# Two decoder blocks in split float32r on one core: pools divided so that matmul operands start at multiples of 128 bytes

## The chip, the cores and the metric

The kernel runs on one NeuronCore of a Trainium2 chip. The metric is the device time of one execution in microseconds (us), as the median of the runs of a kernel. TensorE (PE), VectorE (DVE), ScalarE (ACT) and GpSimd (POOL) compute; SyncE (SP) issues the DMAs.

## The reference

Two transformer blocks follow each other over 256 tokens of width 1024. The first has two layers (a low-rank attention beside a dilated attention, then a block attention), each with a feed-forward part of width 4096 and a gated projection. The second has two layers over the 256 tokens and, in its first layer, 256 context tokens: a gated convolution, an attention and a gated linear attention side by side, three branch projections and an output projection. All of it is float32, and nearly all of the arithmetic is products of a 256-row activation with weight matrices:

```python
h = x
for i in range(DEPTH):
    hn = rms_norm(h, mix_norm[i])
    mix = even_mixer(hn, ...) if i % 2 == 0 else odd_mixer(hn, ...)
...
def odd_mixer(hn, w_in, qn, kn, w_out):
    z = (hn @ w_in).reshape(B, S, 3, MOBA_HEADS, HEAD_DIM)
...
    return o.reshape(B, S, ODD_MIX) @ w_out
```

## The kernel before

**A product in three passes.** Every float32 operand of a large product is held as a pair of float32r tiles, a rounded part `hi` and the remainder `lo`. `mm3` (lines 295 to 299) multiplies a pair by a pair with three matmuls into one PSUM bank, on lines 297, 298 and 299:

```python
        mm(ps, sl, mh, start=first, stop=False)
        mm(ps, sh, ml, start=False, stop=False)
        mm(ps, sh, mh, start=False, stop=last)
```

The second argument of `mm` is the stationary operand (loaded into the array, 128 columns), the third the moving one (streamed through it). The profile names the moving operand first: `mm<-xh,wlo` streams `xh` past the loaded `wlo`.

**Weights.** `unit` (L263) loads up to 1 MB of a weight matrix into a `raw` tile; ACT rounds it into `whi` (L280) and DVE subtracts to get `wlo` (L281), 1024 columns at a time. There are three `raw` buffers and four each of `whi` and `wlo`. PE multiplies one unit while the next ones are loaded and split.

**Two shapes.** `gemm_nat` (L301) keeps a 128x128 piece of the activation stationary and streams 512 (or 384, 288) weight columns; its operands appear as `mm<-whi,xl` and `mm<-wlo,xh`. `gemm_tr` (L326) and `tr_mm` (L286) keep a 128x128 piece of the weight stationary and stream 256 activation columns, `mm<-xh,wlo`. In the second block some weights multiply both token groups at once, with 512 moving activation columns. `branches2` (L1641) is the end of a layer of the second block: it streams `ph` and `pl` (256 columns) past the branch weights, and holds `sh` and `sl` stationary against `w_out_2`.

**Order.** The order of the work is written out by generators: `run` (L1742) interleaves steps of the first block with filler steps of the second by declared costs, and `block2` (L1713) runs the second block's layers. SP issues the weight loads in the order in which PE will use them. This order is fixed when the program is built and does not depend on where a tile lies.

**Where tiles lie.** Every tile comes from a pool, and pools lie one behind another in each partition's memory. Within a pool the tiles lie one behind another, each rounded up to a multiple of 32 bytes. The weight pool `w` comes first and starts at a multiple of 128; each of its tiles is 8192 or 4096 bytes. Next is `const`, which begins with `cols`, 193 floats or 772 bytes, taking 800; everything behind it is shifted by 32 bytes, and further small tiles shift it again. The first block's tiles come from `b1` (and `fill`), the second block's from `d0`, `d1` (`dense2`) and `b0`, `b1` (`branches2`). The start of a tile past a multiple of 128 bytes, in the kernel before:

| tiles | pool | bytes past a multiple of 128 |
|---|---|---|
| `raw`, `whi`, `wlo` | `w` | 0 |
| `ident` | `const` | 32 |
| `xh`, `xl` | `xq` | 64 |
| `E0`, `E1` (in rows: `E`) | first block | 64 |
| `E2`, `E3` (in rows: `E`) | first block | 0 |
| `ph`, `pl`, `sh`, `sl` | `branches2` | 96 |
| `T` tiles, `vvh`, `vvl`, `kTh`, `kTl` | `dense2` | 0, 32, 64 or 96 |

A slice that a matmul reads starts a multiple of 512 bytes inside its tile, so it has the same offset as the tile. Of the large products, `E2` with `E3` against weights has both operands at 0; no product with 256 moving columns has.

Of the kernel before, what the change touches and what calls it, by code (L numbers as in the profile page):

```python
# [10 lines left out]
F32 = mybir.dt.float32  # L11
# [9 lines left out]
P = 128  # L21
# [113 lines left out]
for _n, _k in COLS:  # L135
    COFF[_n] = _o
    _o += _k
NCOL = _o

ROWS = [("e_qn_nope", 64), ("e_qn_rope", 32), ("e_kn_nope", 64), ("e_kn_rope", 32),  # L140
        ("q_norm_g_2", 256), ("k_norm_g_2", 256)]
# [55 lines left out]
        self.hi, self.lo = hi, lo  # L197


class Kern:  # L200
    def __init__(self, tc, ins, out, ctx, dbg=None):
        self.tc, self.nc, self.i, self.out, self.dbg = tc, tc.nc, ins, out, dbg or {}
        pool = lambda n, b, **k: ctx.enter_context(tc.tile_pool(name=n, bufs=b, **k))
        self.wp = pool("w", 3)
        self.cp = pool("const", 1)
        xq = pool("xq", 1)
        self.xs = [xq.tile([P, 2, 8, 256], F32R, name=f"x{n}") for n in "hl"]
        self.zp = pool("zp", 1)
        self.ps = pool("ps", 1, space=PSUM)
        self.nuid = 0  # L210
        self.pre = PRE
# [933 lines left out]
    def evacs(self, l, s, T):  # L1145

        nc, V, A = self.nc, self.nc.vector, self.nc.scalar

        def conv(c):
            st = {}  # L1150

            def e_c(ps):
                st["v"] = T("cv", [P, 2, 256])
                A.copy(st["v"], ps)

            def e_x(ps):
                v = st["v"]
                u = T("cu", [P, 2, 258])
                nc.gpsimd.memset(u[:, :, 0:1], 0.0)
                nc.gpsimd.memset(u[:, :, 257:258], 0.0)  # L1160
                V.tensor_tensor(u[:, :, 1:257], ps, v, op=OP.mult)
                for j in range(2):
                    w = [self.col("conv_w_2", (l * 3 + k) * 8 + c * 2 + j) for k in range(3)]
                    A.mul(v[:, j], u[:, j, 0:256], w[0])
                    V.scalar_tensor_tensor(v[:, j], u[:, j, 1:257], w[1], v[:, j], op0=OP.mult, op1=OP.add)
                    V.scalar_tensor_tensor(v[:, j], u[:, j, 2:258], w[2], v[:, j], op0=OP.mult, op1=OP.add)

            def e_b(ps):
                V.tensor_tensor(st["v"], ps, st["v"], op=OP.mult)

            def e_z(ps):
                z = T("zt", [P, 2, 256])
                A.activation(z, ps, AF.Tanh, scale=0.5)
                V.scalar_tensor_tensor(z, z, 1.0, ps, op0=OP.add, op1=OP.mult)
                V.scalar_tensor_tensor(z, z, 0.5, st["v"], op0=OP.mult, op1=OP.mult)
                self.spill(l, s, "conv", c * 2, z)
            return [(c0 + c * 256, e) for c0, e in ((1024, e_c), (2048, e_x), (0, e_b), (3072, e_z))]

        def silu(name, c):

            def e(ps):
                z = T("zt", [P, 2, 256])
                for o, q in zip([z[:, a] for a in range(2)], ps) if isinstance(ps, list) else [(z, ps)]:
                    A.activation(o, q, AF.Tanh, scale=0.5)
                    V.scalar_tensor_tensor(o, o, 1.0, q, op0=OP.add, op1=OP.mult)
                self.spill(l, s, name, c * 2, z)
            return e

        def gate(j, c):

            def e(ps):
                z = T("zt", [P, 2, 256])
                for a in range(2):
                    A.activation(z[:, a], ps[a] if isinstance(ps, list) else ps[:, a], AF.Tanh, scale=0.5,
                                 bias=self.col("b_gate_2", l * 24 + j * 8 + c * 2 + a))
                self.spill(l, s, f"g{j}", c * 2, z)
            return e
        return {"conv": conv, "silu": silu, "gate": gate}
# [514 lines left out]
    def block2(self, dram, xs_dram):  # L1713
        nc, i = self.nc, self.i
        tc = self.tc
        self.bg, self.credit = [], 0.0
        xp = {0: self.xp0, 1: self.xp1}
        for l in range(2):
            def T(tag, shape, bufs=1, dt=F32):
                self.nuid += 1  # L1720
                return self.dp.tile(shape, dt, name=f"{tag}_{l}_{self.nuid}", tag=tag, bufs=bufs)
            self.rate = RATE[l]
            with tc.tile_pool(name=f"d{l}", bufs=1) as self.dp:
                self.lmask = T("lmask", [P, MASKS, P], dt=I32)
                self.rope2 = T("T9", [P, 2, 2, P])
                nc.sync.dma_start(self.rope2, i["c_rope2"].rearrange("p (c t d) -> p c t d", c=2, t=2))
                nc.sync.dma_start(self.lmask, i["c_lmask"].rearrange("p (a b) -> p a b", a=MASKS))
                mats = self.load(T("T8", [P, 4, P]), i["c_mats"].rearrange("p (a b) -> p a b", a=4))
                self.matsr = T("matsr", [P, 4, P], dt=F32R)
                nc.vector.tensor_copy(self.matsr, mats)  # L1730
                self.dense2(l, xp[0], xp[1])
            with tc.tile_pool(name=f"b{l}", bufs=1) as self.dp:
                ctx_in = self.branch_input(0, 1, 0, T) if l == 0 else None
                x = self.post2(l, 0, *self.branches2(l, 0, T, after=ctx_in), xs_dram[0][l], T, xs_dram[0][l + 1])
                self.dump(f"x{l}", x)
                if l == 0:
                    xp[0] = self.norm2(1, 0, x, T)
                    x = self.post2(0, 1, *self.branches2(0, 1, T, ready=ctx_in), xs_dram[1][0], T)
                    xp[1] = self.norm2(1, 1, x, T)
                    self.conv_units(1, [(0, xp[0])])  # L1740

    def run(self):  # L1742
        nc, i, tc = self.nc, self.i, self.tc
        with tc.tile_pool(name="dram", bufs=1, space=bass.MemoryType.DRAM) as dram:
            tok = lambda a: a.rearrange("(t p) d -> p t d", p=P)
            dt = lambda n: dram.tile([P, 2, D], F32, name=n)
            xs_dram = {0: {0: dt("xl0"), 1: dt("xl1"), 2: tok(self.out)}, 1: {0: tok(i["ctx_2"])}}
            with tc.tile_pool(name="b1", bufs=1) as big, tc.tile_pool(name="fill", bufs=1) as fp:
                self.big, self.fp = big, fp
                self.scr = {(l, s, n): dram.tile([P, 8, 256], F32, name=f"scr{l}{s}{n}")  # L1750
                            for l in range(2) for s in range(2 - l) for n in ("conv", "att", "gla", "za", "zg", "g0", "g1", "g2")}
                self.cz = {n: dram.tile(sh, F32, name=f"cz_{n}") for n, sh in
                           (("k", [P, 2, 512]), ("q", [P, 2, D]), ("gk", [P, 2, 512]), ("gv", [P, 2, D]), ("gq", [P, D]), ("r", [32, 256]))}
                h = self.sb("h", [P, 2, D])
                self.load_consts()
                for b in range(2):
                    for t in range(2):
                        nc.sync.dma_start(h[:, t, b * 512:(b + 1) * 512], tok(i["x"])[:, t, b * 512:(b + 1) * 512])
                    if b == 0:
                        nc.sync.dma_start(self.cols, i["cols"])  # L1760
                        self.first = self.unit(i["e_w_in"], 0, 2, 0, 384)
                self.gdram = [dram.tile([2, D], F32, name=f"gdram{l}") for l in range(2)]

                rest = chain(self.ada(0), self.ada(1))

                def filler():
                    for _ in range(9):
                        yield next(rest)
                    yield from self.ctx_proj(xs_dram[1][0])
                    yield from rest  # L1770
                f = filler()
                turn = 0
                debt = 0.0
                for pe, lat in self.block1(h):
                    if self.ph == "ff0":
                        turn += 1
                        if turn % AT == 0:
                            next(rest, None)
                    debt += lat * LATF
                    while debt > 0:  # L1780
                        d = next(f, None)
                        if d is None:
                            debt = -1e9
                        else:
                            debt -= d
                for _ in f:
                    pass
                nc.sync.dma_start(xs_dram[0][0], h)
            self.block2(dram, xs_dram)
# [21 lines left out]
```

## Time and profile before

| | |
|---|---|
| median of 3 runs | 2135.53 us (2134.28 to 2136.55) |
| the profiled execution | 2133.83 us, of which the span is 2132.1 us |
| PE, matmuls | busy 98% of the span |
| DVE, ACT, POOL | busy 71%, 53%, 0% |
| DMA | 55.4% of 16 engines' time, 186 GB/s in the mean |
| TensorE's granted clock | 0.996 |

The span runs from the first to the last instruction. "Busy" for PE counts a matmul from its start to its modelled end, and matmuls overlap: one of 256 columns lasts some 0.28 us in the profile while the next starts 0.11 us after it. So the busy share says little of how fast PE runs. What counts is the distance from one start to the next, which the timeline shows: the difference between the starts of the first and the last matmul of an unbroken stretch, divided by their number less one. The chain of work that ended last tells which engine's time sets the end.

### The profile page before, as it was taken

Reading aid. Unit: us, or ns where it says so; the run is one execution under the profiler, and the core shown is the slowest. Engines: PE = TensorE matmul, PEld = TensorE weight load, DVE = VectorE, ACT = ScalarE, POOL = GpSimd, SP = SyncE. Lnnn points to the kernel's source line nnn. Section 1 sums busy time; section 2 is a strip of 40 time slices with the busy share of each in tenths; the row PEclk is TensorE's granted clock in tenths of the full one; section 3 lists DMA queues with packets and bytes.
Section 4 is the critical chain, followed back from the end, with each engine's and each line's share of the span. In section 5 each row is a group of like instructions: output and inputs, shape, how many; then the busy total and the mean of one; then the engine's idle time right before and its main releaser. Section 6 shows DMA issues by size and latency. Waiting matters only on the chain.

```text
span 2132.1 us, 34406 instructions
## 1 busy us (share of the span) xinstructions
PE 2092.7 (98%) x13618; PEld 1863.3 (87%) x13618; DVE 1516.2 (71%) x2837; ACT 1120.5 (53%) x1790; POOL 8.4 (0%) x42
## 2 busy tenths in 40 slices
PE   7999999999999999999999999999999999999998
PEld 5788878888999888989998888889899988989997
DVE  6875556677767657998898567347878677668676
ACT  4654434465555445666565545434546445747543
POOL 0000000000000000000000000000000000000000
PEclk9999999999999999999999999999999999999999
DMA  7744687555435555744633343568865631425695
GB/s 265 249 152 166 229 279 275 188 182 189 140 127 178 196 183 193 258 161 139 205 119 118 107 139 113 201 234 276 277 227 192 217 126 65 137 92 159 210 314 178
DMA packets 282154, 397.48 MB, mean 186 GB/s; under 512 B 12676, under 2 KB 189156, under 8 KB 279560
## 3 DMA queue, kind: packets, MB, share of 16 engines
q1 hardware_dynamic: 281992, 395.28, 55.4%
q8 instruction: 107, 1.75, 0.3%
q14 instruction: 55, 0.45, 0.1%
HBM read 363.21 MB, written 32.03 MB: 185 GB/s over the span
## 4 chain that ended last, share of the span: by engine, by line
PE 85%; DVE 6%; DMA 4%; ACT 4%; issue 1%; SPq 0%; DVEq 0%; ACTq 0%
PE mm L298 24%; PE mm L299 24%; PE mm L297 24%; DVE wlo L281 2%; PE tp L1590 2%; DMA raw<-in_w_ff 1%; PE at L1608 1%; PE at L1425 1%; ACT whi L280 1%; PE at L1539 1%; PE at L582 1%; DMA lp<-scr01za 1%; PE tp L1442 1%; PE mm L949 1%; PE at L297 1%
## 5 line engine op out<-in xcount | busy, mean ns | idle before, releaser
L281 DVE TENSOR_TENSOR wlo<-raw,whi 128x1024 fp32r<-128x1024 f32 (+1 forms) x572 | 690.5, 1211 | 321.8 <-ACT whi L280 319.6
L280 ACT CAST whi<-raw 128x1024 fp32r<-128x1024 f32 (+1 forms) x572 | 592.0, 1041 | 487.1 <-PE mm L299 338.2
L297 PE MATMUL mm<-xh,wlo 128*128 128x256 f32 (+2 forms) x2048 | 619.0, 302 | 4.6 <-DVE wlo L281 4.3
L298 PE MATMUL mm<-xl,whi 128*128 128x256 f32 (+2 forms) x2048 | 616.3, 301 | 0.9 <-DVE xl L406 0.9
L299 PE MATMUL mm<-xh,whi 128*128 128x256 f32 (+2 forms) x2048 | 614.7, 300 | 0.0
L297 PEld LDWEIGHTS mm<-xh,wlo 128*128 128x128 f32 (+1 forms) x2048 | 382.6, 187 | 29.1 <-DVE wlo L281 8.3
L299 PEld LDWEIGHTS mm<-xh,whi 128*128 128x128 f32 (+1 forms) x2048 | 383.6, 187 | 14.2
L298 PEld LDWEIGHTS mm<-xl,whi 128*128 128x128 f32 (+1 forms) x2048 | 382.7, 187 | 15.0 <-DVE xl L406 1.1
L298 PE MATMUL mm<-wlo,xh 128*128 128x512 f32 (+3 forms) x704 | 268.7, 382 | 4.4 <-DVE wlo L281 4.4
L297 PE MATMUL mm<-whi,xl 128*128 128x512 f32 (+3 forms) x704 | 267.1, 381 | 4.9 <-ACT whi L280 4.8
L299 PE MATMUL mm<-whi,xh 128*128 128x512 f32 (+3 forms) x704 | 265.9, 378 | 0.0
L297 PE MATMUL mm<-ph,wlo 128*128 128x256 f32 x576 | 162.7, 282 | 0.0
L298 PE MATMUL mm<-pl,whi 128*128 128x256 f32 x576 | 162.6, 282 | 0.0
L299 PE MATMUL mm<-ph,whi 128*128 128x256 f32 x576 | 162.6, 282 | 0.0
L297 PEld LDWEIGHTS mm<-whi,xl 128*128 128x128 f32 x704 | 133.5, 190 | 31.8 <-ACT whi L280 8.0
L298 PEld LDWEIGHTS mm<-wlo,xh 128*128 128x128 f32 x704 | 134.4, 191 | 28.0 <-DVE wlo L281 6.3
L299 PEld LDWEIGHTS mm<-whi,xh 128*128 128x128 f32 x704 | 134.2, 191 | 23.1
L298 PE MATMUL mm<-wlo,E 128*128 128x512 f32 (+1 forms) x292 | 113.7, 389 | 0.6 <-DVE wlo L281 0.6
L297 PE MATMUL mm<-whi,E 128*128 128x512 f32 (+1 forms) x292 | 113.5, 391 | 0.0
L299 PE MATMUL mm<-whi,E 128*128 128x512 f32 (+1 forms) x292 | 113.4, 388 | 0.0
L297 PEld LDWEIGHTS mm<-ph,wlo 128*128 128x128 f32 x576 | 109.2, 190 | 0.2 <-DVE wlo L281 0.2
L298 PEld LDWEIGHTS mm<-pl,whi 128*128 128x128 f32 x576 | 109.3, 190 | 0.1
(449 smaller groups left out, 2827.9 us busy)
## 6 DMA issues: line engine op xcount, KB each, us to landing
raw<-in_w_in SPq DMA_DIRECT2D x130, 1024.0 KB, 5.2
raw<-in_w_ff SPq DMA_DIRECT2D x64, 1024.0 KB, 5.3
raw<-in_w_ada SPq DMA_DIRECT2D x24, 1024.0 KB, 5.6
raw<-in_o_w_in SPq DMA_DIRECT2D x12, 1024.0 KB, 5.0
raw<-in_w_br_conv SPq DMA_DIRECT2D x12, 1024.0 KB, 5.4
raw<-in_w_br_attn SPq DMA_DIRECT2D x12, 1024.0 KB
raw<-in_w_br_gla SPq DMA_DIRECT2D x12, 1024.0 KB, 6.5
raw<-in_w_out SPq DMA_DIRECT2D x12, 1024.0 KB
```

Source lines behind the costliest of these rows:

```text
L280: nc.scalar.copy(hi, src)
L281: nc.vector.tensor_sub(lo, src, hi.bitcast(F32))
L297: mm(ps, sl, mh, start=first, stop=False)
L298: mm(ps, sh, ml, start=False, stop=False)
L299: mm(ps, sh, mh, start=False, stop=last)
L582: nc.tensor.matmul(bank[:, t * P:t * P + nk], qT[:, h, t * P:(t + 1) * P], kT[:, h, :nk], start=True, stop=True)
L949: mm(ps[32 * q:32 * q + 32], self.cpad[:, k0 + k], raw[:, k, b * 512:(b + 1) * 512], start=True, stop=True)
L1425: mm(ps[:, :nk], x[a], y[c], start=n == 0, stop=n == 2)
L1442: tr(tp[:, k * P:(k + 1) * P], e[:, t, k * P:(k + 1) * P], self.ident)
L1539: mm(ps[:, h], ks[:, f, t, h * P:(h + 1) * P], gv[:, t, h * 256:(h + 1) * 256], start=True, stop=True)
L1590: mm(ps[:, j], E[:, 0, j * P:(j + 1) * P], E[:, 1, j * P:(j + 1) * P], start=True, stop=True)
L1608: mm(o, a, c, start=k == 0, stop=k == len(terms) - 1)
```

## The change

Pools are split in two. A new class `Sized` hands a tile to one of two pools: to the `odd` one where the elements of a row are no multiple of 32 (128 bytes of float32), otherwise to the `even` one. It stands in for the pools `const`, `b1`, `fill`, `d0`, `d1` and the second block's `b0` and `b1`. The odd pools lie behind the even ones, so that `even` tiles follow each other without a remainder. A tile `pads` of 9 floats, which nothing reads or writes, makes the size of the pool `small` come out so that the next pool starts at a multiple of 128. The tile `cu` of the convolution grows from 258 to 272 columns a row, of which 258 are used as before. After the change all tiles in the table above start at 0.

All engines issue the same instructions in the same order, and with the same waits, as before; only addresses differ, and the row length of `cu`.

```diff
--- before.py
+++ after.py
@@ -136,6 +136,7 @@
     COFF[_n] = _o
     _o += _k
 NCOL = _o
+PADS = 9
 
 ROWS = [("e_qn_nope", 64), ("e_qn_rope", 32), ("e_kn_nope", 64), ("e_kn_rope", 32),
         ("q_norm_g_2", 256), ("k_norm_g_2", 256)]
@@ -197,15 +198,28 @@
         self.hi, self.lo = hi, lo
 
 
+class Sized:
+
+
+    def __init__(self, even, odd):
+        self.even, self.odd = even, odd
+
+    def tile(self, shape, dt, **k):
+        return (self.odd if math.prod(shape[1:]) % 32 else self.even).tile(shape, dt, **k)
+
+
 class Kern:
     def __init__(self, tc, ins, out, ctx, dbg=None):
         self.tc, self.nc, self.i, self.out, self.dbg = tc, tc.nc, ins, out, dbg or {}
         pool = lambda n, b, **k: ctx.enter_context(tc.tile_pool(name=n, bufs=b, **k))
         self.wp = pool("w", 3)
-        self.cp = pool("const", 1)
+        even = pool("const", 1)
         xq = pool("xq", 1)
         self.xs = [xq.tile([P, 2, 8, 256], F32R, name=f"x{n}") for n in "hl"]
         self.zp = pool("zp", 1)
+        odd = pool("small", 1)
+        self.cp = Sized(even, odd)
+        odd.tile([P, PADS], F32, name="pads")
         self.ps = pool("ps", 1, space=PSUM)
         self.nuid = 0
         self.pre = PRE
@@ -1155,7 +1169,7 @@
 
             def e_x(ps):
                 v = st["v"]
-                u = T("cu", [P, 2, 258])
+                u = T("cu", [P, 2, 272])[:, :, :258]
                 nc.gpsimd.memset(u[:, :, 0:1], 0.0)
                 nc.gpsimd.memset(u[:, :, 257:258], 0.0)
                 V.tensor_tensor(u[:, :, 1:257], ps, v, op=OP.mult)
@@ -1720,7 +1734,8 @@
                 self.nuid += 1
                 return self.dp.tile(shape, dt, name=f"{tag}_{l}_{self.nuid}", tag=tag, bufs=bufs)
             self.rate = RATE[l]
-            with tc.tile_pool(name=f"d{l}", bufs=1) as self.dp:
+            with tc.tile_pool(name=f"d{l}", bufs=1) as even, tc.tile_pool(name=f"d{l}s", bufs=1) as odd:
+                self.dp = Sized(even, odd)
                 self.lmask = T("lmask", [P, MASKS, P], dt=I32)
                 self.rope2 = T("T9", [P, 2, 2, P])
                 nc.sync.dma_start(self.rope2, i["c_rope2"].rearrange("p (c t d) -> p c t d", c=2, t=2))
@@ -1729,7 +1744,8 @@
                 self.matsr = T("matsr", [P, 4, P], dt=F32R)
                 nc.vector.tensor_copy(self.matsr, mats)
                 self.dense2(l, xp[0], xp[1])
-            with tc.tile_pool(name=f"b{l}", bufs=1) as self.dp:
+            with tc.tile_pool(name=f"b{l}", bufs=1) as even, tc.tile_pool(name=f"b{l}s", bufs=1) as odd:
+                self.dp = Sized(even, odd)
                 ctx_in = self.branch_input(0, 1, 0, T) if l == 0 else None
                 x = self.post2(l, 0, *self.branches2(l, 0, T, after=ctx_in), xs_dram[0][l], T, xs_dram[0][l + 1])
                 self.dump(f"x{l}", x)
@@ -1745,8 +1761,9 @@
             tok = lambda a: a.rearrange("(t p) d -> p t d", p=P)
             dt = lambda n: dram.tile([P, 2, D], F32, name=n)
             xs_dram = {0: {0: dt("xl0"), 1: dt("xl1"), 2: tok(self.out)}, 1: {0: tok(i["ctx_2"])}}
-            with tc.tile_pool(name="b1", bufs=1) as big, tc.tile_pool(name="fill", bufs=1) as fp:
-                self.big, self.fp = big, fp
+            with tc.tile_pool(name="b1", bufs=1) as big, tc.tile_pool(name="fill", bufs=1) as fp, \
+                    tc.tile_pool(name="b1s", bufs=1) as odd:
+                self.big, self.fp = Sized(big, odd), Sized(fp, odd)
                 self.scr = {(l, s, n): dram.tile([P, 8, 256], F32, name=f"scr{l}{s}{n}")
                             for l in range(2) for s in range(2 - l) for n in ("conv", "att", "gla", "za", "zg", "g0", "g1", "g2")}
                 self.cz = {n: dram.tile(sh, F32, name=f"cz_{n}") for n, sh in
```

## Rows read from the trace of the kernel before

**Rows 1.** Granted clock (view of cores); busy time by engine (page, part 1).

```profile
core 0: 2132.1 us, clock 0.996
...
PE 2092.7 (98%) x13618; PEld 1863.3 (87%) x13618; DVE 1516.2 (71%) x2837; ACT 1120.5 (53%) x1790; POOL 8.4 (0%) x42
```

**Rows 2.** The chain that ended last (page, part 4): by engine, then by line.

```profile
PE 85%; DVE 6%; DMA 4%; ACT 4%; issue 1%; SPq 0%; DVEq 0%; ACTq 0%
PE mm L298 24%; PE mm L299 24%; PE mm L297 24%; DVE wlo L281 2%; PE tp L1590 2%; DMA raw<-in_w_ff 1%; PE at L1608 1%; PE at L1425 1%; ACT whi L280 1%; PE at L1539 1%; PE at L582 1%; DMA lp<-scr01za 1%; PE tp L1442 1%; PE mm L949 1%; PE at L297 1%
```

**Rows 3.** PE by form, L297: xcount | busy us, mean ns | idle.

```profile
L297 PE MATMUL mm<-xh,wlo 128*128 128x256 f32 x1696 | 479.1, 283 | 4.6 <-DVE wlo L281 4.3 <-ACT xh L405 0.3
...
L297 PE MATMUL mm<-whi,xl 128*128 128x512 f32 x576 | 228.5, 398 | 2.6 <-ACT whi L280 2.5
...
L297 PE MATMUL mm<-ph,wlo 128*128 128x256 f32 x576 | 162.7, 282 | 0.0
...
L297 PE MATMUL mm<-xh,wlo 128*128 128x512 f32 x320 | 131.0, 409 | 0.0
...
L297 PE MATMUL mm<-whi,E 128*128 128x512 f32 x280 | 109.5, 393 | 0.0
...
L297 PE MATMUL mm<-whi,sl 128*128 128x512 f32 x96 | 37.9, 395 | 0.0
...
L297 PE MATMUL mm<-whi,xl 128*128 128x256 f32 x96 | 27.4, 285 | 0.0
...
L297 PE MATMUL at<-T,vvl 128*128 128x256 f32 x80 | 24.2, 302 | 0.4
```

**Rows 4.** Timeline of PE, first and last of 96: start us, length us, instruction.

```profile
420.08 0.39 PE L297 MATMUL mm<-whi,E 128*128 128x512 f32 x1
...
441.62 0.39 PE L299 MATMUL mm<-whi,E 128*128 128x512 f32 x1
```

**Rows 5.** Timeline of PE, first and last of 288.

```profile
478.98 0.40 PE L297 MATMUL mm<-whi,xl 128*128 128x512 f32 x1
...
544.70 0.40 PE L299 MATMUL mm<-whi,xh 128*128 128x512 f32 x1
```

**Rows 6.** Timeline of PE, first and last of 284.

```profile
1359.54 0.39 PE L298 MATMUL mm<-xl,whi 128*128 128x512 f32 x1
...
1425.57 0.40 PE L299 MATMUL mm<-xh,whi 128*128 128x512 f32 x1
```

**Rows 7.** Timeline of PE, first and last of 67.

```profile
1493.96 0.39 PE L297 MATMUL mm<-whi,sl 128*128 128x512 f32 x1
...
1509.36 0.40 PE L297 MATMUL mm<-whi,sl 128*128 128x512 f32 x1
```

**Rows 8.** Timeline of PE, first and last of 576.

```profile
1425.81 0.28 PE L297 MATMUL mm<-ph,wlo 128*128 128x256 f32 x1
...
1493.85 0.27 PE L299 MATMUL mm<-ph,whi 128*128 128x256 f32 x1
```

**Rows 9.** Timeline of PE, first and last of 375.

```profile
647.70 0.28 PE L299 MATMUL mm<-xh,whi 128*128 128x256 f32 x1
...
690.09 0.28 PE L299 MATMUL mm<-xh,whi 128*128 128x256 f32 x1
```

**Rows 10.** Timeline of PE, first and last of 192.

```profile
375.48 0.28 PE L297 MATMUL mm<-xh,wlo 128*128 128x256 f32 x1
...
397.97 0.28 PE L299 MATMUL mm<-xh,whi 128*128 128x256 f32 x1
```

**Rows 11.** Waits of PE, longest in total: us, times, longest.

```profile
PE tp L402 <- DMA h<-in_x: 7.1, 2, 4.5
PE mm L298 <- DVE wlo L281: 5.6, 7, 2.1
```

**Rows 12.** Groups of DVE by form, two of one shape.

```profile
L281 DVE TENSOR_TENSOR wlo<-raw,whi 128x1024 fp32r<-128x1024 f32 x558 | 679.7, 1222 | 317.0 <-ACT whi L280 314.8 <-issue 0.3
L1583 DVE TENSOR_TENSOR T<-T,kq 128x1024 f32<-128x1024 f32 x42 | 51.2, 1219 | 1.0 <-ACT T L1582 0.6
```


## The prediction

> **What bounds the kernel now.** I read the shares of busy time first, then the chain, then the starts of matmuls in the timeline. PE holds a busy matmul 98% of the span, at a granted clock of 0.996, so practically all of the time at the upper level of 2.4 GHz [rows 1]. The chain says the same in a stricter way: 85% of the time that sets the end is PE's, and the three lines of `mm3` alone have 72% [rows 2]. PE hardly ever stands idle: its longest wait in total is 7.1 us at the very start, the next 5.6 us [rows 11]. So the kernel is a stream of matmuls, and what counts is how soon one follows another. The mean length of a matmul in the groups (283 ns for 256 columns) is no measure of that, since neighbours overlap; the groups are used for their counts alone [rows 3].
>
> The distance from start to start comes from unbroken stretches of the timeline. I chose stretches in which nothing but one form runs, and divided the difference of the first and last start by the number of steps.
>
> - Both operands at offset 0, 512 moving columns (`E2`, `E3` against weights): 21.54 us over 95 steps, 226.7 ns [rows 4].
> - Stationary `xh`/`xl` at 64, moving weights at 0, 512 columns: 65.72 us over 287, 229.0 ns [rows 5].
> - Moving `xh`/`xl` at 64, stationary weights at 0, 512 columns: 66.03 us over 283, 233.3 ns [rows 6].
> - Stationary `sh`/`sl` at 96, moving weights at 0, 512 columns: 15.40 us over 66, 233.3 ns [rows 7].
> - Moving `ph`/`pl` at 96, 256 columns: 68.04 us over 575, 118.3 ns [rows 8].
> - Moving `xh`/`xl` at 64, 256 columns: either 42.39 us over 374, 113.3 ns [rows 9], or 22.49 us over 191, 117.7 ns [rows 10]. The same tiles at the same offset run at either pace, and a stretch keeps the pace that it has found.
>
> So equal shapes take unequal times, and the order follows the offsets. Half of the aligned 226.7 is 113.4, the quick pace of the 256-column form. That is why I take 226.7 ns for 512 columns and 113.4 ns for 256 as what is left when both operands start at 0. For 256 columns this is an inference, as no row has both at 0.
>
> Here a rule speaks against the change. The Trainium skill, page "SBUF — State Buffer", section "Specifications (TRN2)", gives the memory lines of 16 bytes. All offsets here are multiples of 32, so by that rule every tile begins on a line of its own already, and the change would save nothing. The rows disagree with that reading (226.7 against 229.0 and 233.3), so something coarser than 16 bytes matters; the sum goes by the rows.
>
> **The change part by part.** It adds and removes no instruction, no wait and no DMA; `pads` is never touched. It moves every operand of the large products to offset 0. Each of rows 3 stands for three lines of equal count. Gains:
>
> - 512 columns, stationary at 64: 576 x 3 = 1,728 of `xh`/`xl`, and 432 of the 840 with `E` (the others are `E2`/`E3`, at 0 already). 2,160 x (229.0 - 226.7) = 5.0 us [rows 3 to 5].
> - 512 columns, moving at 64: 320 x 3 = 960 x 6.6 ns = 6.3 us [rows 3, 6].
> - 512 columns, stationary at 96: 96 x 3 = 288 x 6.6 = 1.9 us [rows 3, 7].
> - 256 columns, moving at 96: 576 x 3 = 1,728 x (118.3 - 113.4) = 8.5 us [rows 3, 8].
> - 256 columns, moving at 64: 1696 x 3 = 5,088. Of the eleven unbroken stretches of more than 70 such matmuls, seven (1,994 matmuls) run at the pace of rows 9 and four (544) at that of rows 10. So 21% lose 4.4 ns: 5,088 x 0.21 x 4.4 = 4.7 us [rows 3, 9, 10].
> - The smaller forms `mm<-whi,xl` with 256 columns and `at<-T,vvl`: (96 + 80) x 3 = 528, at the same 4.4 ns as the nearest row: 2.3 us [rows 3, 10].
>
> Together 28.7 us. How much of that reaches the end? Where PE's time is on the chain, all of it; where the chain runs through DVE, ACT or a DMA, a quicker PE only waits longer, first of all in `mm` on L297 and L298 for `wlo` of DVE L281, which is the wait that grows [rows 2, 11]. With PE's 85% the lower bound is 24.4 us; the upper is the full 28.7. I take the middle, 26.6: the chain changes sides for a unit at a time, and PE's waits are short, so part of the 15% will be regained.
>
> The rest I price at nothing. DVE and ACT do the same instructions: DVE's 128x1024 subtraction takes 1222 ns on tiles at 0 and 1219 ns on `T` tiles, which lie at other offsets, so an operand's place does not matter to it [rows 12]. The small tiles behind feed instructions of a few columns, off the chain's large shares. `cu` is written by POOL, which is idle. The weight loads land in tiles that stay at 0. Loads into the tiles that move (`lp` from the spilled branches) hold 1% of the chain, 21 us [rows 2]; no row shows the same load at two offsets, so I take zero, with 2 us either way for the range.
>
> The profiled execution took 2133.83 us, 1.7 below the median of the three runs. It becomes 2107.2; against the median, 2135.5 - 26.6 = 2108.9, which I call 2109.
>
> **The rivals.**
>
> *The 256-column streams keep two paces.* The pace of rows 9 and 10 differs at one and the same offset, so it could hang on how a stream begins and not on the offset. Then the 5,088 gain nothing, `ph` falls to the mixed mean of 114.3 only (1,728 x 4.0 = 6.9 us), the smaller forms give 1.8, and the 512-column forms give their 13.2: 21.9 us, of which with the chain's share about 20 arrive: 2115.5. For it: rows 9 and 10. Against it: with both operands at 0 the 512-column form stays at 226.7 through all of its 96 steps [rows 4], and the forms at 96 or with 512 moving columns at 64 never fall to the low pace in the stretches read. Chance 0.20.
>
> *Offsets do not matter; the forms differ for another reason.* The rows compare different tiles in different stages. If `sh` is slow because of what else runs in its stage, moving it does nothing: 2135.5. The 16-byte rule cited above would give this result. Against it: rows 6 and 8 adjoin in time and both miss the low pace, while rows 4 and 10 lie some 20 us apart and differ in kind. Chance 0.05.
>
> *Both operands at 0 get in each other's way at 256 columns.* The stationary read of the next matmul and the moving read of this one now start at the same place in a 128-byte step, in every pair. If that locks all 256-column streams at the fixed pace of `ph`, 118.3 ns [rows 8], the 5,088 lose 118.3 - 114.3 = 4.0 ns each, 20.4 us, against 13.2 us that the 512-column forms gain: 7.2 us slower, 2143. It decides from 117.3 ns on: the 6,816 matmuls of the two large 256-column forms now average 115.3, and 13.2 us divided among them are 1.9 ns. For it: no 256-column row has both at 0. Against it: rows 4 have both at 0 and are the quickest of their shape. Chance 0.04.
>
> *The streams reach the array's own pace.* At 2.4 GHz 512 columns at one a cycle are 213.3 ns, and rows 4 stand 13.4 ns above that. Were that rest also an effect of offsets, the 3,816 matmuls of 512 columns would gain another 13.4 ns and the 7,344 of 256 another 6.7: 100 us, some 85 on the chain, so about 2024. Against it: rows 4 already have what the change brings, and keep the 13.4. Chance 0.02. The Trainium skill, page "TensorE: Matmul & The Clock Gate", section "Back-to-back issue gap", gives a distance of N/2.4 + 2.5 ns, 215.8 for 512 columns and 109.2 for 256; the time by it would be about 2046 as an estimate from that page, and rows 4 speak against it for these float32r products.
>
> **How the numbers follow.** The forecast has 0.69, the rivals 0.20, 0.05, 0.04 and 0.02. A difference of 0.2%, about 4.3 us, is what a measurement of this kernel can tell from none. Faster by more than that: 0.69 + 0.20 + 0.02 = 0.91; within it 0.05; slower 0.04. The forecast's own range is 2106.8 (all of 28.7) to 2111.1 (85%); with the 2 us of the loads and the starts of stretches, which I left out of the counts, it reaches down to 2101. The first rival with 85% of its gain, and 2 us of loads, ends at 2119. So 2101 to 2119.
>
> **What would show it.** In the changed profile the stretch of `ph` should step at 113.4 ns and end some 2.8 us sooner after its start; the 512-column streams of rows 5, 6 and 7 should all step at 226.7; 256-column stretches at 117.7 should be gone. DVE L281 should stay near 1222 ns, and PE's waits for `wlo` should grow by a few us. The prediction is wrong if 256-column streams still show 117 or more (first or third rival), if nothing changes (second), if a 512-column stream steps below 226 ns (fourth), or if the steps shrink as said and the time does not, in which case waits for `wlo` or `raw` have taken their place.

## The result: slower by 0.7%, and the profile after

The changed kernel takes 2149.57 us as the median of 4 runs (2148.80 to 2150.82), the kernel before 2134.91 us on the same chip (2132.48 to 2136.55). The ratio is 1.007 (95% interval 1.0058 to 1.0082). 2109 us was forecast, in a range of 2101 to 2119.

First the cores view of the changed kernel, then parts 1 and 4 of its page (busy time by engine; the chain by engine). Its lines of the program stand 14 further down: L311 to L313 are `mm3`, L295 is the subtraction.

```profile
core 0: 2147.0 us, clock 0.997
```

```profile
PE 2111.1 (98%) x13618; PEld 1888.2 (88%) x13618; DVE 1518.0 (71%) x2837; ACT 1121.2 (52%) x1790; POOL 8.4 (0%) x42
...
PE 88%; DVE 5%; DMA 3%; ACT 2%; issue 1%; SPq 0%; DVEq 0%; ACTq 0%
```

The span has grown by 14.9 us, at the same clock and with the same counts of instructions. PE's share of the chain rose from 85% to 88%, so the time is PE's own [rows 1, 2]. The group of the subtraction (by form) and PE's longest waits in total (us, times, longest) exclude the other engines:

```profile
L295 DVE TENSOR_TENSOR wlo<-raw,whi 128x1024 fp32r<-128x1024 f32 x558 | 679.9, 1221 | 330.7 <-ACT whi L294 328.2 <-DMA raw<-in_w_in 0.6 <-issue 0.3
```

```profile
PE tp L416 <- DMA h<-in_x: 7.3, 2, 4.6
PE mm L312 <- DVE wlo L295: 5.1, 5, 2.4
```

The subtraction lasts 1221 ns against 1222 [rows 12], and PE waits no longer than before [rows 11]. What remains is the pace of the matmuls. This is the timeline of PE in the changed kernel, in pairs of first and last matmul: the stretches that answer to rows 5, 6, 8, 7, 9 and 10, then 96 products of weights with `E0`/`E1`, and at last the last stretch of `ph`/`pl`:

```profile
481.74 0.40 PE L311 MATMUL mm<-whi,xl 128*128 128x512 f32 x1
546.82 0.39 PE L313 MATMUL mm<-whi,xh 128*128 128x512 f32 x1
...
1369.97 0.39 PE L312 MATMUL mm<-xl,whi 128*128 128x512 f32 x1
1434.13 0.39 PE L313 MATMUL mm<-xh,whi 128*128 128x512 f32 x1
...
1434.36 0.28 PE L311 MATMUL mm<-ph,wlo 128*128 128x256 f32 x1
1503.35 0.29 PE L313 MATMUL mm<-ph,whi 128*128 128x256 f32 x1
...
1503.47 0.40 PE L311 MATMUL mm<-whi,sl 128*128 128x512 f32 x1
1518.87 0.40 PE L311 MATMUL mm<-whi,sl 128*128 128x512 f32 x1
...
649.89 0.28 PE L313 MATMUL mm<-xh,whi 128*128 128x256 f32 x1
694.76 0.28 PE L313 MATMUL mm<-xh,whi 128*128 128x256 f32 x1
...
377.54 0.28 PE L311 MATMUL mm<-xh,wlo 128*128 128x256 f32 x1
400.46 0.28 PE L313 MATMUL mm<-xh,whi 128*128 128x256 f32 x1
...
694.88 0.39 PE L311 MATMUL mm<-whi,E 128*128 128x512 f32 x1
716.94 0.39 PE L313 MATMUL mm<-whi,E 128*128 128x512 f32 x1
...
2048.51 0.28 PE L311 MATMUL mm<-ph,wlo 128*128 128x256 f32 x1
2116.74 0.28 PE L313 MATMUL mm<-ph,whi 128*128 128x256 f32 x1
```

The same 96 products with `E0`/`E1` in the kernel before:

```profile
690.20 0.39 PE L297 MATMUL mm<-whi,E 128*128 128x512 f32 x1
711.95 0.39 PE L299 MATMUL mm<-whi,E 128*128 128x512 f32 x1
```

| stretch | steps | before, ns | after, ns |
|---|---|---|---|
| 512 columns, `xh`/`xl` stationary [rows 5] | 287 | 229.0 | 65.08 / 287 = 226.8 |
| 512, `xh`/`xl` moving [rows 6] | 283 | 233.3 | 64.16 / 283 = 226.7 |
| 512, `sh`/`sl` stationary [rows 7] | 66 | 233.3 | 15.40 / 66 = 233.3 |
| 512, `E0`/`E1` stationary | 95 | 21.75 / 95 = 228.9 | 22.06 / 95 = 232.2 |
| 256, `ph`/`pl` moving [rows 8] | 575 | 118.3 | 68.99 / 575 = 120.0 |
| 256, `ph`/`pl` moving, the last stretch | 575 | 118.3 | 68.23 / 575 = 118.7 |
| 256, `xh`/`xl` moving [rows 9] | 374 | 113.3 | 44.87 / 374 = 120.0 |
| 256, `xh`/`xl` moving [rows 10] | 191 | 117.7 | 22.92 / 191 = 120.0 |

Two rows came out as forecast, the first two. `sh` and `sl` stayed where they were in this stretch, `E0` and `E1` got slower, and the `xh`/`xl` streams of 256 columns all fell to 120.0 ns: in the unbroken stretches of 20 matmuls or more, 3,418 of 4,578 stepped at 113 to 114 ns before and the others at 118, and all 4,578 at 120 after. `ph`/`pl` did not: of their three long stretches one steps at 120.0, the others at 118.9 (1544.26 to 1598.46 us) and 118.7.

Adding up the distance to the next start over all matmuls of a kind gives the balance: 3,912 of 512 columns went from 931.3 to 924.0 us (7.3 gained), 7,680 of 256 columns from 945.9 to 969.1 (23.1 lost), all others gained 0.9. That is 14.9 us of loss, as much as the span grew. Of the 23.1 us, 22.8 are those of `xh`/`xl` (615.0 to 637.8 us). The sum for `ph`/`pl` stayed (208.8 to 208.5): their steps take 119.2 ns in the mean after 118.3, and the gaps between their stretches shrank.

### The profile page after: what moved, and what is told of

Its sections match the earlier page's. It is cut to its first block, busy times and chain, and to the rows that moved or that the text cites. A ratio compares the mean times of both kernels' runs of the same rounds, so it can differ in the third digit from the quotient of the medians.

```text
span 2147.0 us, 34406 instructions
## 1 busy us (share of the span) xinstructions
PE 2111.1 (98%) x13618; PEld 1888.2 (88%) x13618; DVE 1518.0 (71%) x2837; ACT 1121.2 (52%) x1790; POOL 8.4 (0%) x42
## 4 chain that ended last, share of the span: by engine, by line
PE 88%; DVE 5%; DMA 3%; ACT 2%; issue 1%; SPq 0%; DVEq 0%; ACTq 0%
PE mm L312 25%; PE mm L313 25%; PE mm L311 25%; DVE wlo L295 2%; PE tp L1604 2%; DMA raw<-in_w_ff 2%; PE at L1622 1%; PE at L1439 1%; PE at L1553 1%; PE at L596 1%; ACT whi L294 1%; PE tp L1456 1%; PE mm L963 1%; PE at L311 1%; PE tp L570 1%
## 5 line engine op out<-in xcount | busy, mean ns | idle before, releaser
L295 DVE TENSOR_TENSOR wlo<-raw,whi 128x1024 fp32r<-128x1024 f32 (+1 forms) x572 | 690.8, 1211 | 335.8 <-ACT whi L294 333.3
L311 PE MATMUL mm<-xh,wlo 128*128 128x256 f32 (+2 forms) x2048 | 625.9, 306 | 3.9 <-DVE wlo L295 3.6
L312 PE MATMUL mm<-xl,whi 128*128 128x256 f32 (+2 forms) x2048 | 623.3, 304 | 0.9 <-DVE xl L420 0.9
L313 PE MATMUL mm<-xh,whi 128*128 128x256 f32 (+2 forms) x2048 | 621.8, 304 | 0.0
L311 PEld LDWEIGHTS mm<-xh,wlo 128*128 128x128 f32 (+1 forms) x2048 | 388.3, 190 | 26.8 <-DVE wlo L295 7.7
L312 PEld LDWEIGHTS mm<-xl,whi 128*128 128x128 f32 (+1 forms) x2048 | 388.6, 190 | 13.6 <-DVE xl L420 1.1
L313 PEld LDWEIGHTS mm<-xh,whi 128*128 128x128 f32 (+1 forms) x2048 | 388.5, 190 | 12.7
L311 PE MATMUL mm<-whi,xl 128*128 128x512 f32 (+3 forms) x704 | 265.9, 380 | 4.3 <-ACT whi L294 4.1
L313 PE MATMUL mm<-whi,xh 128*128 128x512 f32 (+3 forms) x704 | 265.1, 377 | 0.0
L313 PE MATMUL mm<-ph,whi 128*128 128x256 f32 x576 | 163.0, 283 | 0.0
L311 PE MATMUL mm<-ph,wlo 128*128 128x256 f32 x576 | 162.1, 281 | 0.0
L311 PEld LDWEIGHTS mm<-whi,xl 128*128 128x128 f32 x704 | 133.6, 191 | 30.1 <-ACT whi L294 7.3
L313 PEld LDWEIGHTS mm<-whi,xh 128*128 128x128 f32 x704 | 134.5, 191 | 22.1
L312 PE MATMUL mm<-wlo,E 128*128 128x512 f32 (+1 forms) x292 | 114.1, 391 | 0.3 <-DVE wlo L295 0.3
L313 PE MATMUL mm<-whi,E 128*128 128x512 f32 (+1 forms) x292 | 113.9, 390 | 0.0
L311 PE MATMUL mm<-whi,E 128*128 128x512 f32 (+1 forms) x292 | 113.9, 392 | 0.0
L311 PEld LDWEIGHTS mm<-ph,wlo 128*128 128x128 f32 x576 | 108.8, 189 | 0.1
L313 PEld LDWEIGHTS mm<-ph,whi 128*128 128x128 f32 x576 | 108.6, 188 | 0.0
```

What stands on the lines that cost most here:

```text
L295: nc.vector.tensor_sub(lo, src, hi.bitcast(F32))
```

## Experiments

The tiles that all start at a multiple of 128 bytes after the change do not all start at the same place in 256 bytes: `xh`/`xl` and `E2`/`E3` lie at the place of the weights, `E0`/`E1`, `ph`/`pl` and `sh`/`sl` lie 128 bytes from it. The theory was therefore that what counts is the distance between the starts of the stationary and the moving operand, taken modulo 256 bytes. The rival was that each operand's own start counts.

**Streams alone, every pair of offsets.** A kernel of matmuls only, on the same split operands, 48 in a stream of 256 columns and 24 in one of 512; `a` moves the moving and `b` the stationary operand in steps of 32 bytes, and the whole is gone through twice, the second time in reverse.

```python
mm(ps[:, :256], sta[:, b + k * P:b + (k + 1) * P], mov[:, a + k * 256:a + (k + 1) * 256], ...)
...
mm(ps, sta[:, b + k * 256:b + k * 256 + P], mov[:, a + k * 512:a + (k + 1) * 512], ...)
```

> It leaves out the whole computation: streams of float32r matmuls alone, 48 with 256 moving columns and 24 with 512, for moving operands that start 0 to 224 bytes (letter 1, in steps of 32) and stationary operands that start 0 to 224 bytes (letter 2; for moving 0 up to 992) past a common multiple, each twice, the second time in reverse order. No other engine works beside them. Theory A, the two operands' starts against each other: with 256 columns 120 ns wherever both start at the same place, at whatever offset, and about 113 at some distances between them, 64 bytes among them; with 512 columns 227 at equal starts and 229 to 233 at others. Theory B, the moving operand's own start: with 256 columns 120 ns for every stationary offset while the moving one starts at 0, and 113 to 118 at 64. Theory C, other engines' and DMA traffic in the stage: no difference between any offsets here, all at one pace.

Measured, as mean distance of starts in the second half of a stream (both rounds where they differ):

| distance, bytes | 0 | 32 | 64 | 96 | 128 | 160 | 192 | 224 |
|---|---|---|---|---|---|---|---|---|
| 256 columns, ns | 120.0 | 118.4 | 113.3 / 117.8 | 117.3 / 118.9 | 118.7 (119.9 twice) | 119.9 | 117.8 (113.3 once) | 116.6 to 117.9 |
| 512 columns, ns | 226.6 | 233.3 | 233.3 | 234.4 | 233.0 | 233.5 | 228.7 | 233.2 |

The eight moving offsets that share a distance (stationary less moving, modulo 256) agree nearly everywhere within 0.5 ns; where 256 columns show two values, the rounds or the pairs of one distance differ. Going on to 992 bytes the table repeats every 256. Timeline of this kernel, first and last of a stream (in a name the first letter is the form, n for 256 and w for 512 columns, the second the moving and the third the stationary offset, a for 0, c for 64, e for 128):

```profile
223.18 0.28 PE L45 MATMUL ncc<-xh,wl 128*128 128x256 f32 x1
228.81 0.28 PE L45 MATMUL ncc<-xh,wh 128*128 128x256 f32 x1
...
245.68 0.28 PE L45 MATMUL nce<-xh,wl 128*128 128x256 f32 x1
251.01 0.28 PE L45 MATMUL nce<-xh,wh 128*128 128x256 f32 x1
...
228.93 0.40 PE L51 MATMUL wcc<-wh,xl 128*128 128x512 f32 x1
234.17 0.40 PE L51 MATMUL wcc<-wh,xh 128*128 128x512 f32 x1
...
206.48 0.39 PE L51 MATMUL wca<-wh,xl 128*128 128x512 f32 x1
211.74 0.40 PE L51 MATMUL wca<-wh,xh 128*128 128x512 f32 x1
```

`ncc` has both operands at 64, at no multiple of 128, and steps at 5.63 / 47 = 119.8 ns; `nce` has one at 64 and one at 128 and steps at 5.33 / 47 = 113.4. With 512 columns it is the other way round: `wcc` 5.24 / 23 = 227.8, `wca`, which is 192 apart, 5.26 / 23 = 228.7, and the second halves 226.6 and 229.0. So it is the distance, and the two forms want different distances. The table also gives the kernel before: `xh` stationary was 192 from the weights (228.7; 229.0 in rows 5), `sh` 224 (233.2; 233.3 in rows 7), `xh` moving 64 (233.3 and 113.3 / 117.8; the same in rows 6, 9 and 10), `ph` 32 (118.4; 118.3 in rows 8). After the change `xh` is at 0 (226.6 and 120.0), `sh` and `E0` at 128 (233.0; 233.3 and 232.2). `ph`, at 128 too, takes both paces that the streams show there: 118.7 and 118.9, near their usual 118.7, and once 120.0, near the 119.9 that they show twice.

Both operands were moved in steps of 32 bytes here, and all stationary slices of a stream lie at one place modulo 256. So no run tells whether the moving operand meets the slice that it multiplies or the one that is loaded for the next matmul.

**Undo one part: `xh` and `xl` back at their old distance.** From the changed kernel, 48 floats ahead of `xq`, the other operands 128 bytes further, which brings `sh`/`sl`, `E0`/`E1` and `ph`/`pl` to a distance of 0 from the weights and `E2`/`E3` to 128.

```diff
+        pool("gap", 1).tile([P, 48], F32, name="gap")
         xq = pool("xq", 1)
...
-        odd.tile([P, PADS], F32, name="pads")
```

> The changed kernel with xh and xl alone shifted back to 64 past a multiple of 128 (as before the change, also to 256), by a gap of 48 floats ahead of them and without the 9 floats of pads; the other matmul operands stay at multiples of 128, though 128 bytes further on. Theories A and B: the x-fed streams of 256 columns return to 113.3 or 117.7 ns, those of 512 to 229.0 and 233.3, so about 26 us back and 10 us lost: 2134 us, between 2130 and 2138. Theory C: nothing changes, 2149.6 us. If the distance between the two starts matters up to 256 bytes and not 128, the streams of E0 and E1 and of sh, which the 128 bytes move, change from 232 to 227 ns as well.

Measured: 2138.53 us (10 runs) against 2133.55 before, ratio 1.0018 (1.0009 to 1.0028). Some 11 us of the loss come back, and the median lies half a microsecond above the range that was expected. One long stretch shows the main reason. Timeline of PE, the same 379 matmuls, in the kernel before:

```profile
860.13 0.28 PE L299 MATMUL mm<-xh,whi 128*128 128x256 f32 x1
902.98 0.28 PE L299 MATMUL mm<-xh,whi 128*128 128x256 f32 x1
```

and with `xh` back at its old distance:

```profile
858.09 0.28 PE L313 MATMUL mm<-xh,whi 128*128 128x256 f32 x1
902.61 0.28 PE L313 MATMUL mm<-xh,whi 128*128 128x256 f32 x1
```

42.85 / 378 = 113.4 ns there, 44.52 / 378 = 117.8 here, at the same distance of 64. Both paces of rows 9 and 10 are back, but the slower one has more of the matmuls: 2,325 of the 4,578 against 1,160 in the kernel before. `ph`, now at a distance of 0, steps at 120.0 ns in all of its long stretches. `sh`/`sl`, at 0 as well, step faster in a stretch of 96, timeline of PE:

```profile
1593.44 0.40 PE L311 MATMUL mm<-whi,sl 128*128 128x512 f32 x1
1615.00 0.39 PE L313 MATMUL mm<-whi,sh 128*128 128x512 f32 x1
```

That is 21.56 / 95 = 226.9 ns, where the changed kernel has 232.3. `E0`/`E1` fall from 232.3 to 226.8 in a stretch of 96, and `E2`/`E3`, now at 128, rise from 226.9 to 232.2 in another. So a move by 128 bytes changes the pace: what counts is the distance modulo 256 and not modulo 128.

**Finer distances.** The kernel of streams again, with one operand fixed and the other moved by 0 to 252 bytes in steps of 4, in three orders.

```diff
-    grid = [(m, s) for m in range(8) for s in range(8)]
-    return grid + [(0, s) for s in range(8, 32)]
+    return [(0, s) for s in range(0, 64)]
...
-                a, b = m * 8, s * 8
+                a, b = m, s
```

> It leaves out the whole computation: as the run scan, streams of 48 matmuls with 256 moving columns and 24 with 512, the moving operand always at 0 and the stationary one 0 to 252 bytes on in steps of 4 (letter 1: steps of 32 bytes, letter 2: of 4), three times: in rising, falling and mixed order. Theory A, the distance of the two starts up to 256 bytes sets the pace: at the multiples of 32 the paces of the run scan (256 columns: 120.0 at 0, 118.4 at 32, 113.3 or 117.8 at 64; 512 columns: 226.6 at 0, near 233 elsewhere, 228.6 at 192). Between them, if it is a matter of the distance as such, values that change from step to step; if of whole 32-byte pieces that are read, flat steps. Rival D, that the low pace at 64 is a matter of how a stream begins and could come at any distance: 113.3 then shows at other distances too in some of the three orders.

Measured: with 256 columns 120.0 ns at a distance of 0, 118.3 at 4, 115.6 at 8, 123.2 at 204, and between 113.3 and 121.7 elsewhere. A rule that counts lines of 16 bytes does not decide alone, since 4, 8 and 12 bytes lie in one such line and have 118.3, 115.6 and 116.9. 512 columns show 226.6 at 0, 120, 132, 156 and 240 and mostly 230 to 234 elsewhere, 239.1 at worst. At 52, 64, 88, 168 and 192 bytes the three orders give 113.3 in some rounds and 116.7 to 120.0 in others, as rival D has it; at 76 all three give 113.3. No distance gives both forms their shortest step, 113.3 and 226.6. Timeline of PE, the second round at 76 (5.36 / 47 = 114.0 with the entry into the stream, 113.3 in its second half):

```profile
1238.46 0.28 PE L44 MATMUL ncd<-xh,wl 128*128 128x256 f32 x1
1243.82 0.28 PE L44 MATMUL ncd<-xh,wh 128*128 128x256 f32 x1
```

**A distance for each form.** The changed kernel, with the weights put where each form wants them: 0 from the activations for 512 columns, 64 bytes for 256 columns. The weight tiles grow to 1088 floats; small tiles `ea`, `eb` and `pb` of 32 floats bring `E0`/`E1` and the tiles of `branches2` to the weights' place in 256 bytes, and two masks move from `const` to `b1` to make room. Units whose products stream both token groups (512 columns) get `off=0`. Only the lines on the weights are shown:

```diff
+                o = off if off is not None else 16 if tr else 48 if n == 256 else 0
...
-                ...name=f"w{a}{u}_{k0}_{n0}", tag=f"w{a}", bufs=4)[:, :kk * wide]
+                ...name=f"w{a}{u}_{k0}_{n0}", tag=f"w{a}", bufs=4)[:, o:o + kk * wide]
```

> The changed kernel with distances chosen by the run scan: weight tiles are 64 floats longer, and units that stand still while 256 columns stream lie 64 bytes into their tile, so that the stationary start is 64 bytes past the moving one (256-column natural units: 192 bytes into it, the same distance); all 512-column products have both at the same start up to 256 bytes (E0, E1, ph, pl, sh, sl moved by 128 bytes). Two masks move to the first block's pool to make room. Theory A: 256-column streams at 113.3 or 117.7 ns, mean 113.4 to 114.7 in place of 119.7, 7,000 of them: 35 to 44 us back; E0, E1 and sh from 232 to 227, 4 us: 2149.6 less 39 to 48 is 2102 to 2111 us. Theory B (own start of the moving operand at a multiple of 128 is slow for 256 columns): they stay at 120, about 2145 us.

Measured: 2124.30 us (5 runs) against 2134.89 before, ratio 0.995 (0.9934 to 0.9966): faster than both kernels, but short of what was expected. Timeline of PE:

```profile
1418.56 0.28 PE L312 MATMUL mm<-ph,wlo 128*128 128x256 f32 x1
1486.29 0.28 PE L314 MATMUL mm<-ph,whi 128*128 128x256 f32 x1
1486.40 0.40 PE L312 MATMUL mm<-whi,sl 128*128 128x512 f32 x1
1501.39 0.39 PE L312 MATMUL mm<-whi,sl 128*128 128x512 f32 x1
...
1527.88 0.28 PE L312 MATMUL mm<-ph,wlo 128*128 128x256 f32 x1
1579.45 0.28 PE L314 MATMUL mm<-ph,whi 128*128 128x256 f32 x1
```

The streams of 512 columns now step at 227 ns (`sl`: 14.99 / 66 = 227.1). The 256-column streams take either: 67.73 / 575 = 117.8 in one stretch of `ph`, 51.57 / 455 = 113.3 in the next. The slower one has 2,531 of the 4,578 matmuls with `xh`/`xl`, more than twice the 1,160 of the kernel before, and that is the main reason why the gain fell short.

**The same, with a distance of 0 for 256 columns.**

```diff
-                o = off if off is not None else 16 if tr else 48 if n == 256 else 0
+                o = off if off is not None else 0 if tr else 0 if n == 256 else 0
```

> The kernel of the run dist with the distance taken back to 0 in the 256-column products; its longer weight tiles, the masks' other pool and the 128-byte moves of E0, E1, ph and sh stay. Theory A: 256-column streams at 120 ns again, 512-column ones at 227; the changed kernel's 2149.6 less 4 us for E0, E1 and sh: 2145 us, about 21 above dist. If the gain of dist came from its other moves, it stays at 2124 us.

Measured: 2147.10 us (4 runs) against 2132.85 before, ratio 1.0058 (1.0036 to 1.0079). The same `ph` stretch, timeline of PE:

```profile
1432.70 0.28 PE L312 MATMUL mm<-ph,wlo 128*128 128x256 f32 x1
1501.69 0.28 PE L314 MATMUL mm<-ph,whi 128*128 128x256 f32 x1
```

It steps at 68.99 / 575 = 120.0. Between this kernel and the last there is nothing but the place of the weights for one form, and the ratios lie 1.1% apart, some 23 us. All 4,578 matmuls with `xh`/`xl` step at 120 again. That a distance of 0 is the cause of the loss is thus shown within the whole kernel.

**The same, with 76 bytes.**

```diff
-                o = off if off is not None else 16 if tr else 48 if n == 256 else 0
+                o = off if off is not None else 19 if tr else 45 if n == 256 else 0
```

> The kernel of the run dist with a distance of 76 bytes in place of 64 in the 256-column products (natural units: 180 bytes into the tile, the same distance). Theory A with the run scan2, in which 76 gave 113.3 ns in all three orders and 64 gave both paces: all x-fed and ph-fed streams of 256 columns run at 113.3 ns, none at 117.8; 18 us come back from the 2124.3 of dist, so about 2106 us. Rival D (the low pace is a matter of how a stream begins, at any distance): 256-column stretches at 113.3 and at 117.8 beside each other as in dist, about 2124 us.

Measured: 2122.45 us (5 runs) against 2132.85 before, ratio 0.9943 (0.9926 to 0.9961). Of this kernel: the timeline of PE, PE's longest wait in total (us, times, longest), and the chain by engine:

```profile
1417.19 0.28 PE L312 MATMUL mm<-ph,wlo 128*128 128x256 f32 x1
1482.37 0.28 PE L314 MATMUL mm<-ph,whi 128*128 128x256 f32 x1
...
1526.48 0.28 PE L312 MATMUL mm<-ph,wlo 128*128 128x256 f32 x1
1581.08 0.28 PE L314 MATMUL mm<-ph,whi 128*128 128x256 f32 x1
```

```profile
PE mm L313 <- DVE wlo L296: 7.5, 8, 1.9
```

```profile
PE 82%; DVE 7%; DMA 6%; ACT 4%; issue 2%; SPq 0%; DVEq 0%; ACTq 0%
```

The first `ph` stretch has 65.18 / 575 = 113.4, as nearly all others; the second has 54.60 / 455 = 120.0, where 64 bytes gave 113.3. Beside that, a quicker PE begins to wait: 7.5 us for `wlo` against 5.6 [rows 11], and 82% of the chain against 85 [rows 2]. The interval overlaps that of 64 bytes, so the two kernels cannot be told apart by their times, and 2106 us was not reached: in the two traces the steps of `xh`/`xl` and `ph`/`pl` take 10.8 us less than with 64 bytes, and the span is 4.1 us shorter.

The distance is not the whole rule, either. The 288 products in which 256 weight columns move past `xh`/`xl` have the same distance of 76 bytes, but their moving operand starts 180 bytes into its tile, which is no multiple of 32. Their first and last matmul in one stretch of 21, timeline of PE:

```profile
1768.35 0.28 PE L313 MATMUL mm<-wlo,xh 128*128 128x256 f32 x1
1770.81 0.28 PE L312 MATMUL mm<-whi,xl 128*128 128x256 f32 x1
```

They step at 2.46 / 20 = 123.0 ns here and at 119.9 in the longest stretch of 36, where 64 bytes gave 114.1 and 117.8, and nowhere at 113.3. So for starts that are no multiple of 32 bytes the distance alone does not give the pace; no run takes that further.

**What chooses between the paces.** Streams of 96 matmuls at distances of 0, 64 and 76 bytes, each behind eight matmuls of 32 to 512 columns, in two rounds, the second in reverse.

```python
for q in range(8):
    mm(ps[:, :cols], x[q % 2][:, q * 256:q * 256 + P], w[0][:, :cols], start=q == 0, stop=q == 7)
```

> It leaves out the whole computation: streams of 96 float32r matmuls with 256 moving columns at distances of 0 (letter a), 64 (b) and 76 bytes (c) between the two operands' starts, each begun behind 8 matmuls of 32, 64, ... 512 columns (letter 2, a to p), twice, the second time in reverse order. Theory A with a choice at the beginning (rival D's part that is left): at 64 the stream runs at 113.3 behind some beginnings and at 117.8 behind others, and keeps that pace for all of its 96; at 76 nearly all are at 113.3 and a few at 120; at 0 all are at 120. If the distance alone sets the pace, each distance has one pace behind all 16 beginnings; if the beginning alone does, the three distances show the same mixture.

Measured: at 0 all 32 streams step at 120.0; at 64, 18 at 113.3 and 14 at 117.8; at 76, 29 at 113.3 and 3 at 120.0. Each keeps its pace from its second quarter to its end. Timeline of PE (in a name the second letter is the distance, a for 0, b for 64, c for 76, the third the columns ahead, f for 192):

```profile
214.29 0.30 PE L46 MATMUL nbf<-xh,wl 128*128 128x256 f32 x1
225.10 0.28 PE L46 MATMUL nbf<-xh,wh 128*128 128x256 f32 x1
...
1001.52 0.30 PE L46 MATMUL nbf<-xh,wl 128*128 128x256 f32 x1
1012.73 0.28 PE L46 MATMUL nbf<-xh,wh 128*128 128x256 f32 x1
```

`nbf` is one and the same stream at the same addresses: 10.81 / 95 = 113.8 ns in the first round, 11.21 / 95 = 118.0 in the second. Behind 384 columns the stream at 64 bytes steps at 117.8 in both rounds. Behind eight matmuls of 256 columns or more, the two rounds at 64 agree for 9 lengths of 9; behind shorter ones for 1 of 7. So, with the moving operand at one place, the distance sets which paces there are, and the beginning of the stream which of them it takes. What about the beginning decides is left open.

## Why the prediction was wrong

- **What bounds the kernel** was right: PE's stream of matmuls, and the distance of starts as the quantity to read. No other engine's time moved, and the loss arrived in full, 14.9 us by the starts and 14.9 in the span. The discount of 85 to 100% for the chain had no part in it.
- **The step that failed** is the price of 256 columns: "Half of the aligned 226.7 is 113.4, the quick pace of the 256-column form. That is why I take 226.7 ns for 512 columns and 113.4 ns for 256 as what is left when both operands start at 0." Both at 0 is 120.0 ns for 256 columns, slower than any of rows 8 to 10 (118.3 at most). So instead of the 8.5 + 4.7 + 2.3 = 15.5 us that were to be gained, 23.1 were lost, 22.8 of them by `xh`/`xl`. The term of 8.5 us for `ph`/`pl` failed by the distance as well: they came to 128 bytes from the weights, not to 0, and step at 119.2 ns in the mean in place of 113.4. The two forms were taken to follow one rule, where the streams alone show opposite ones: a distance of 0 is best for 512 columns and nearly the worst for 256.
- **The gain of 512 columns** was predicted at 13.2 us and came to 7.3. `xh` and `xl` took the paces that the sum had for them (226.8 and 226.7) and gained 7.3 of its 10.3 us; the other 3 us are missing in the short stretches and the gaps around them, which the prices from long stretches do not cover. The offsets ahead of the prediction are modulo 128, and that was too short: `sh`, `sl`, `E0` and `E1` ended 128 bytes from the weights' place in 256, so that `sh` and `sl` gained 0 to 1.0 ns in a step in place of 6.6, and `E0` and `E1` lost 3.3 ns each.
- **The chance of a loss** was the third rival's 0.04 alone, and the range ended at 2119, although no row had both operands at 0 with 256 columns, as the text itself says. That rival had the right condition, the two operands' starts at the same place in every pair; whether they get in each other's way in reading, as it says, no run shows. Its price, 118.3 ns, was too low by 1.7, and its 2143 us lie 6.6 below the 2149.57 measured. "Against it: rows 4 have both at 0 and are the quickest of their shape" was the inference from 512 columns once more.
- **The first rival**, that 256-column streams keep two paces at one offset, is true at distances of 64 and 76, and of 128, where `ph`/`pl` went; but `xh`/`xl` went to 0, at which there is one.
- **The 16-byte rule** of the Trainium skill, page "SBUF — State Buffer", section "Specifications (TRN2)", was set aside rightly, but in favour of a coarser grain alone; the streams show a finer one as well (118.3 ns at 4 bytes, 115.6 at 8).
- **The fourth rival** came to nothing: no stream settled below 226.6 and 113.3 ns. The formula that it takes from the Trainium skill, page "TensorE: Matmul & The Clock Gate", section "Back-to-back issue gap", is meant there for an isolated matmul, not for a stream with a load for each.
- The parts priced at nothing were so: DVE at 1221 ns, PE's waits at 7.3 and 5.1 us. One reason given was not right: POOL writes only the edge columns of `cu`, and DVE writes the others (DVE busy 1518.0 us after 1516.2).

## What to carry to other kernels

Read the distance from start to start for each form of matmul, and relate it to the distance between the two operands' starts modulo 256 bytes, not to the alignment of either to 128. Before aligning everything, measure each form alone: no place of the weights among the 64 tried gives both 256 and 512 moving columns their shortest step, and 64 bytes between the operands of one form instead of 0 were worth 1.1% here. Where a price is inferred from another shape, leave room for the other sign.

## What the runs showed of the hardware

- The pace of float32r matmuls with a new weight load each time depends on the two starts' distance with a period of 256 bytes, shown for starts at multiples of 32 bytes, and from 4 to 4 bytes with the moving operand at one place: 113.3 to 123.3 ns for 256 columns, 226.6 to 239.1 for 512. No stream settled below 113.3 and 226.6 at a granted clock of 0.999 to 1.000.
- At some distances a stream settles at its beginning on one of two paces and keeps it, over 576 matmuls in one case (117.8 at 64 bytes). So two kernels with the same distance in one stage can differ by 4% there, as 113.4 and 117.8 ns over the same 379 matmuls did.
- PE's weight loads were busy longer too: 13,618 of them for 1888.2 us after the change and 1863.3 before [rows 1]. That the loads and the streams disturb each other in reading would fit, but no run here separates the two, and the cause behind the distance stays open.
